# Splitting fp32 weights in tiles of 2048 columns instead of 1024, in a one-core transformer layer

## The chip, the cores and the metric

The kernel runs on one core of one Trainium2 chip. Its engines are TensorE (PE in the profile; PEld is its weight load), VectorE (DVE), ScalarE (ACT), GpSimd (POOL) and SyncE (SP), which issues most DMAs. Each engine takes its own instructions in the order in which they stand in the program, and waits at semaphores for the others. The metric is the device time of one execution in microseconds, lower is better; the time before is the median of three runs.

## The reference

One layer on 256 tokens of 2048 numbers, in fp32, batch 1, depth 1:

```python
x = x + 0.5 * swiglu(rmsnorm(x, ffn1_norm), ffn1_w_gate, ffn1_w_up, ffn1_w_down)   # 2048 -> 5632 -> 2048
h = rmsnorm(x, mix_norm)
rq, rk, rv, rg, aq, ak, av, iq, ik, iw = split(h @ w_in)
ro = group_norm(retention(rope(rq), rope(rk), rv)) * ret_norm * silu(rg)            # 8 heads of 128
ao = sparse_attention(rope(aq), rope(ak), av, rope(iq), rope(ik), iw)               # 8 heads, 64 keys of 256 kept
x = x + concat([ro, ao]) @ w_out
x = x + 0.5 * swiglu(rmsnorm(x, ffn2_norm), ffn2_w_gate, ffn2_w_up, ffn2_w_down)
return rmsnorm(x, final_norm)
# swiglu(h, g, u, d) = (silu(h @ g) * (h @ u)) @ d
```

All weights are fp32 and are read once from HBM, 356 MB in all.

## The kernel before

**Two halves of a number.** A product of fp32 matrices is made of three matmuls on rounded numbers: each operand is split into `hi` (the number rounded by a ScalarE copy to the type fp32r) and `lo` (the number minus `hi`, a VectorE subtraction), and hi·hi, hi·lo and lo·hi are summed in PSUM. So every weight that comes from HBM passes one copy on ScalarE (line 283) and one subtraction on VectorE (line 289) before TensorE can use it.

**Pairs.** A wide matrix product takes its weights in pairs: 256 rows by 1024 columns, laid out as one tile `raw` of 128 partitions by 2048 columns, that is four blocks of 512 columns; one DMA of 1 MB brings it (line 262). Three `raw` tiles exist, so a load waits until the tile three loads back has been read for the last time. A pair is of one of two kinds:

- A **C pair** is multiplied as it is: 4 blocks x 2 token halves x 3 = 24 matmuls of 512 columns.
- An **S pair** uses a scheme with seven products of 2 x 2 blocks instead of eight (the names A11, S1 to S4, M1 to M7 in the code): 7 x 3 = 21 matmuls. For it VectorE first makes four differences of blocks in place in `raw` (`less`, line 275), and the left operand needs sums of its blocks too (`blocks_of`).

The letters of `UP`, `PLAIN` and `DOWN` say which pairs are of which kind. In the order of execution the eight pairs of a usual chunk are S C S C S C C C.

**Stages.** Each FFN has 11 chunks (c0 to c10) of 512 gate and 512 up columns with 8 pairs each; c0 has C pairs alone. After c0 to c5 comes a first down part: 12 pairs for each of two halves d0 and d1 of the output; after c6 to c10 a second one with 10 pairs for each half. Between the FFNs stand the input projections of the mixer (`stream`, `cols`), its attention and retention, and w_out as two wide products, of which the first has three S pairs. At the end of a chunk the sums of the seven products are put together on VectorE (`sums_of`, `ups`, `hidden`; lines 473 and 555) with two SiLUs on ScalarE (line 552); eight TensorE transposes in the next chunk turn the result, and `left_pair` splits it for the down part.

**What sets the order.** The program is written out piece by piece. A piece is a part of a pair: two for a C pair, four for an S pair. The last loop of `layer` runs over the pieces: it calls `split` for pieces up to four ahead, then `run_step` (whatever `after` has put at that step, the sums and transposes among it), then the matmuls of the piece. The engines keep that order. Before the change `split` makes for each piece one `hi` and one `lo` tile of 1024 columns, of five each in turn:

```python
hi = new(wts, [P, 1024], F32R, "hi", BUFS)
lo = new(wts, [P, 1024], F32R, "lo", BUFS)
S.activation(hi[:, :p["n"]], raw, AF.Copy)
...
V.tensor_tensor(lo[:, :p["n"]], raw, hi[:, :p["n"]].bitcast(F32), op=OP.subtract)
```

In an S pair the four differences are put between these: one before the second piece's copy, two before its subtraction, one before the third piece's subtraction.

**Other places that the change touches.** `tables` makes the sine and cosine tables of the rotary embedding during the first down part of the first FFN: some 17 VectorE instructions for each of two tables, with `yield n` for "go on n pieces later". `turn_late` transposes the second half of x for the next stage. `cols("iq", ...)` is the first of the mixer's projections. `FIRST_SQ` and `first_x` belong to the start, where the pairs of x are split as they arrive.

Of the kernel before, what the change touches and what calls it, by code (L numbers as in the profile page):

```python
# [11 lines left out]
F32 = mybir.dt.float32  # L12
# [19 lines left out]
DOWN = ("SCSCSCSCCCCC", "SCSCSCSCCC")  # L32
# [5 lines left out]
BUFS = 5  # L38
# [12 lines left out]
def layer(ctx: ExitStack, tc: tile.TileContext, a: dict, out: bass.AP):  # L51
# [5 lines left out]
    mid = ctx.enter_context(tc.tile_pool(name="mid", bufs=16))  # L57
# [97 lines left out]
    def mm_rows(chunk, n, kts, rhs, first, last):  # L155
# [21 lines left out]

    def wide(src, plan, left, x0=False, tail=False, order=None, sums=SUM):
# [15 lines left out]
        for at, p in enumerate(order or range(len(plan))):  # L194
# [6 lines left out]
            if kind == "C":  # L201
                tiles = [(0, 1024), (1024, 1024)]
                if x0 and at == 0:
                    tiles = [(0, 512), (512, 512), (1024, 1024)]
            else:
                tiles = [(512, 1024), (1024, 1024), (0, 1024), (1536, 512)]
            for k, (off, n) in enumerate(tiles):
                pieces.append(dict(load=len(loads) - 1, off=off, n=n, mms=[], left=left, pair=p,
                                   sums=k if kind == "S" else None, x=[p] if x0 and k == 0 else []))
# [10 lines left out]
            else:  # L220
                for k, off, a, m in S_BLOCKS:
                    mm(i + k, off, a, m)
# [18 lines left out]
    def stream(src, kts, width, per_load, per_piece, rhs, chunk, maker, arg):  # L241

        n = len(kts)
        for l0 in range(0, n, per_load):
            l1 = min(n, l0 + per_load)
            loads.append([(0, block(src, l0, l1, width))])
            for k0 in range(l0, l1, per_piece):
                k1 = min(l1, k0 + per_piece)
                pieces.append(dict(load=len(loads) - 1, off=(k0 - l0) * width, n=(k1 - k0) * width,
                                   mm=maker(chunk, arg, kts[k0:k1], rhs, k0 == 0, k1 == n)))  # L250
# [12 lines left out]

    def split(i):
# [7 lines left out]
        raw = r[:, p["off"]:p["off"] + p["n"]]  # L272
# [249 lines left out]
    def ffn(which, norm, next_norm, last):  # L522
        wgu, wd = a[f"wgu{which}"], [a[f"wd{which}{j}"] for j in range(2)]
        c = 0
        for part, n in enumerate(PARTS):
            hs = {}
            marks[which, part] = len(pieces)
            for cc in range(n):
                plain = c == 0
                start, s_end, half, end = wide(wgu[c], PLAIN if plain else UP, left_of(xg if plain else xs),  # L530
                                               plain and which == 1, order=None if plain else ORDER)
# [41 lines left out]
            for d in range(2):  # L573
# [18 lines left out]
    def turn_late(end, norm, banks):  # L592

        for i, s in ((2, 0), (3, 0), (0, 1), (1, 1)):
            after(end + s, lambda i=i: turn_x(4 + i, norm, banks[i]))
# [49 lines left out]
    def tables():  # L645
        for k in range(2):
# [3 lines left out]
            yield 3  # L650
# [45 lines left out]
    after(marks[1, 0, "down"] + 6, tables)  # L696
# [60 lines left out]
    cols("iq", a["w_iq"], 4, True)  # L757
# [347 lines left out]
def _pairs(w, plans):  # L1105
# [3 lines left out]
    order = {"S": ((0, 1), (0, 0), (1, 1), (1, 0)), "C": ((0, 1), (1, 1), (0, 0), (1, 0))}  # L1109
    return np.stack([np.concatenate([np.stack([chunk[p][:, kt, c] for kt, c in order[plan[p]]], 1).reshape(-1)  # L1110
                                     for p in (ORDER if plan is UP else range(len(plan)))])
                     for chunk, plan in zip(t, plans)])


def _layout(i):
# [22 lines left out]
    arr["w_out"] = c(_pairs(np.concatenate([wo[D // 2:], wo[:D // 2]]), [UP, PLAIN]))  # L1138
# [18 lines left out]
```

## Time and profile before

| | |
|---|---|
| time, median of 3 runs | 1871.88 us (1871.86 to 1872.03) |
| the profiled execution: its time, its span | 1873.38 us, 1871.6 us |
| TensorE matmul busy | 1838.7 us (98%), 8643 matmuls |
| VectorE busy | 1647.2 us (88%) |
| ScalarE busy | 1074.0 us (57%) |
| subtractions (line 289), copies (line 283) | 859, 977.2 us; 859, 846.3 us |
| differences (line 275) | 380, 262.9 us |
| HBM read | 356 MB, 192 GB/s over the span |

The span is what the profiler recorded of one execution; some microseconds lie around it. "Busy" of TensorE is modelled at the matmuls' ends, so a stage's length and number of matmuls tell more than its share. "ACT hi L283" in a list of waits is the copy, "DVE lo L289" the subtraction; "<-" behind an idle time names what ended it.

### The profile page before, as it was taken

What the parts mean: (1) busy time and instruction counts of PE and PEld (TensorE: products, weight loads), DVE (VectorE), ACT (ScalarE), POOL (GpSimd) and SP (SyncE); (2) the same over time, 40 slices, a digit from 0 to 9 for tenths busy, and PEclk for the clock granted to TensorE, in tenths of its full rate; (3) what the DMA queues carried; (4) which work ended last, traced back from release to release, by engine and by line L of the source; (5) the groups of instructions that cost most, each with busy time, mean ns of one, the idle gap of its engine ahead of it and who ended that gap; (6) DMA issues with size and microseconds to landing.
All of it is one profiled execution on the core that took longest, in us unless ns stands there. A gap on an engine that the chain in (4) does not pass through costs nothing.

```text
span 1871.6 us, 22796 instructions
## 1 busy us (share of the span) xinstructions
PE 1838.7 (98%) x8643; PEld 1524.3 (81%) x8643; DVE 1647.2 (88%) x2122; ACT 1074.0 (57%) x1353; POOL 5.8 (0%) x15
## 2 busy tenths in 40 slices
PE   9999998999999999999999999999999999999997
PEld 7888786788888887888888888888888888888886
DVE  7999999989999997789865886799999889999997
ACT  7655554455555555656554565555565455565564
POOL 0000000000000000000000000000000000000000
PEclk9999999999999999999999999999999999999999
DMA  8545555555555454545444454554554555545454
GB/s 317 201 180 197 193 200 186 185 199 206 182 212 212 184 204 165 183 158 206 179 156 158 157 209 154 205 198 181 206 210 182 209 197 195 194 183 213 189 190 170
DMA packets 52365, 360.51 MB, mean 193 GB/s; under 512 B 5984, under 2 KB 5984, under 8 KB 9760
## 3 DMA queue, kind: packets, MB, share of 16 engines
q1 hardware_dynamic: 50976, 355.62, 51.2%
q10 hardware_dynamic: 864, 2.13, 0.3%
q8 instruction: 67, 1.10, 0.2%
q0 software_dynamic: 416, 1.32, 0.2%
q14 instruction: 42, 0.34, 0.1%
HBM read 356.42 MB, written 2.62 MB: 192 GB/s over the span
## 4 chain that ended last, share of the span: by engine, by line
PE 83%; DVE 11%; ACT 3%; issue 1%; DMA 1%; ACTq 0%; SPq 0%; DVEq 0%
PE M L235 66%; PE M L149 8%; DVE lo L289 6%; PE M L151 4%; ACT hi L283 2%; DVE raw L275 2%; PE M L562 1%; PE M L168 1%; PE M L167 1%; PE M L166 1%; DVE x L470 1%; DMA e<-in_xT 0%; PE M L820 0%; ACT sq L412 0%; DVE e L473 0%
## 5 line engine op out<-in xcount | busy, mean ns | idle before, releaser
L283 ACT ACTIVATE hi<-raw 128x1024 fp32r<-128x1024 f32 (+2 forms) x859 | 846.3, 1007 | 558.1 <-DVE raw L275 360.9
L289 DVE TENSOR_TENSOR lo<-raw,hi 128x1024 fp32r<-128x1024 f32 (+2 forms) x859 | 977.2, 1159 | 129.6 <-ACT hi L283 116.4
L235 PE MATMUL M<-hi,xg 128*128 128x512 f32 x2240 | 726.0, 390 | 0.2 <-ACT hi L283 0.2
L235 PE MATMUL M<-hi,mid 128*128 128x512 f32 x1690 | 529.1, 391 | 2.8 <-DVE e L987 1.6
L235 PEld LDWEIGHTS M<-hi,xg 128*128 128x128 f32 x2240 | 420.5, 188 | 87.4 <-ACT hi L283 0.4
L235 PE MATMUL M<-lo,xg 128*128 128x512 f32 x1120 | 437.9, 391 | 5.6 <-DVE lo L289 5.6
L235 PEld LDWEIGHTS M<-hi,mid 128*128 128x128 f32 x1690 | 317.9, 188 | 71.7 <-DVE e L987 2.0
L235 PE MATMUL M<-lo,mid 128*128 128x512 f32 x845 | 330.4, 391 | 4.5 <-DVE lo L289 4.5
L275 DVE TENSOR_TENSOR raw<-raw 128x512 f32<-128x512 f32 x380 | 262.9, 692 | 12.7
L235 PEld LDWEIGHTS M<-lo,xg 128*128 128x128 f32 x1120 | 210.3, 188 | 55.0 <-DVE lo L289 12.2
L149 PE MATMUL M<-xg,hi 128*128 128x512 f32 x688 | 244.5, 399 | 1.2 <-DVE xg L303 1.2
L235 PEld LDWEIGHTS M<-lo,mid 128*128 128x128 f32 x845 | 159.0, 188 | 40.4 <-DVE lo L289 8.1
L151 PE MATMUL M<-xg,lo 128*128 128x256 f32 x645 | 180.5, 280 | 0.0
L149 PEld LDWEIGHTS M<-xg,hi 128*128 128x128 f32 x688 | 128.2, 188 | 30.9 <-DVE xg L303 1.8
L235 PE MATMUL M<-hi,ext 128*128 128x512 f32 x360 | 141.2, 392 | 0.1
L151 PEld LDWEIGHTS M<-xg,lo 128*128 128x128 f32 x645 | 121.8, 189 | 0.7
L235 PEld LDWEIGHTS M<-hi,ext 128*128 128x128 f32 x360 | 67.5, 188 | 17.2 <-DVE s L473 3.7
L235 PE MATMUL M<-lo,ext 128*128 128x512 f32 x180 | 70.1, 390 | 0.0
L473 DVE TENSOR_TENSOR s<-s,M 128x512 f32<-128x512 f32 x98 | 65.6, 683 | 1.9 <-PE M L235 0.9
L552 ACT ACTIVATE s<-s,r_tok 128x512 f32<-128x512 f32 x40 | 27.1, 719 | 53.7 <-DVE s L473 53.7
L473 DVE TENSOR_TENSOR e<-s,M 128x512 f32<-128x512 f32 x58 | 39.7, 684 | 1.0
L734 ACT ACTIVATE b<-e 64x512 f32<-64x512 f32 (+2 forms) x46 | 28.2, 612 | 20.2 <-DVE e L720 19.7
(175 smaller groups left out, 933.6 us busy)
## 6 DMA issues: line engine op xcount, KB each, us to landing
raw<-in_wgu SPq DMA_DIRECT2D x175, 1024.0 KB, 4.8
raw<-in_wd SPq DMA_DIRECT2D x88, 1024.0 KB, 4.8
raw<-in_w_out SPq DMA_DIRECT2D x16, 1024.0 KB, 4.8
raw<-in_w_iq SPq DMA_DIRECT2D x8, 1024.0 KB, 4.8
raw<-in_w_aq SPq DMA_DIRECT2D x8, 1024.0 KB, 4.8
raw<-in_w_rk SPq DMA_DIRECT2D x8, 1024.0 KB, 4.9
raw<-in_w_rq SPq DMA_DIRECT2D x8, 1024.0 KB, 4.8
raw<-in_w_rv SPq DMA_DIRECT2D x8, 1024.0 KB, 4.8
```

The costliest lines, as they stand in the source:

```text
L149: TE.matmul(acc, lhsT=hi[:, c:c + P], rhs=r, start=st, stop=sp)
L151: TE.matmul(acc[:, T:], lhsT=lo[:, c:c + P], rhs=r[:, :T], start=False, stop=False)
L166: TE.matmul(o, lhsT=h, rhs=hi[:, i * n:(i + 1) * n], start=st, stop=False)
L167: TE.matmul(o, lhsT=h, rhs=lo[:, i * n:(i + 1) * n], start=False, stop=False)
L168: TE.matmul(o, lhsT=l, rhs=hi[:, i * n:(i + 1) * n], start=False, stop=sp)
L235: TE.matmul(bank[m], lhsT=p["left"](pair, a)[u], rhs=split_of[i][v][:, off:off + 512], start=st, stop=sp)
L275: V.tensor_tensor(r[:, o:o + 512], r[:, a:a + 512], r[:, b:b + 512], op=OP.subtract)
L283: S.activation(hi[:, :p["n"]], raw, AF.Copy)
L289: V.tensor_tensor(lo[:, :p["n"]], raw, hi[:, :p["n"]].bitcast(F32), op=OP.subtract)
L473: V.tensor_tensor(o, a, b, op=OP.add)
L552: S.activation(u[b], bank[SUM[b]] if plain else u[b], AF.Silu, scale=r_tok[norm][:, t:t + 1])
L734: S.activation(b[p0:p0 + w], q[p1:p1 + w], AF.Copy)
```

## The change

Line numbers of the kernel after are larger: the copy is L274, the subtraction L275, the difference L303, the sums L497, the SiLU L577 and the products behind it L580.

- `split` keeps `hi` and `lo` tiles of 2048 columns, three each in turn: one of each for a C pair, two for an S pair. A C pair gets two copies of 1024 columns and one subtraction of 2048. An S pair gets first two copies (1024 and 512) and one subtraction of 1536 columns, then all four differences, two copies of 1024 and one subtraction of 2048.
- `S_BLOCKS` names the tile that each of the seven products reads; the piece in which its matmuls stand is as before but for two that change places.
- The first down part has five S pairs among its twelve instead of four; the left operands take 17 `mid` buffers instead of 16.
- At the start, chunk c0 of the first FFN takes its pairs in the order FIRST, those that are C in later chunks first.
- `tables` has longer steps between its instructions and starts 5 pieces earlier; its results leave by a POOL DMA.
- The first two index chunks take their loads in turns, and `turn_late` runs one piece later before the mixer.
- The program is built with 4096 bytes of dynamic DMA scratch.

```diff
-DOWN = ("SCSCSCSCCCCC", "SCSCSCSCCC")
+FIRST = (0, 2, 4, 6, 7, 1, 3, 5)
+DOWN = ("SCSCSCSCSCCC", "SCSCSCSCCC")
-BUFS = 5
+AHEAD = 4
-    mid = ctx.enter_context(tc.tile_pool(name="mid", bufs=16))
+    mid = ctx.enter_context(tc.tile_pool(name="mid", bufs=17))
     S_BLOCKS = (
-        (0, 0, "A11", "M1"), (0, 512, "S4", "M3"),
-        (1, 0, "S3", "M7"), (1, 512, "A12", "M2"),
...
+        (0, 0, 512, "A11", "M1"), (0, 0, 1024, "S4", "M3"),
+        (1, 0, 1536, "A12", "M2"), (1, 1, 1024, "S3", "M7"),
...
-                tiles = [(512, 1024), (1024, 1024), (0, 1024), (1536, 512)]
+                tiles = [(0, 2048)] * 4
...
+    def halves_of(r, hi, lo, a, b):
+
+        for o in range(a, b, 1024):
+            S.activation(hi[:, o:min(b, o + 1024)], r[:, o:min(b, o + 1024)], AF.Copy)
+        V.tensor_tensor(lo[:, a:b], r[:, a:b], hi[:, a:b].bitcast(F32), op=OP.subtract)
+
+    def parts(key):
+        if key not in split_in:
+            split_in[key] = [new(wts, [P, 2048], F32R, h, 3) for h in ("hi", "lo")]
+        return split_in[key]
...
-        raw = r[:, p["off"]:p["off"] + p["n"]]
+        k = p.get("sums")
+        if k is None:
+            hi, lo = parts(p["load"])
+            a, b = p["off"], p["off"] + p["n"]
+            if not p.get("second"):
+                halves_of(r, hi, lo, a, 2048 if p.get("whole") else b)
+            split_of[i] = (hi[:, a:b], lo[:, a:b])
+            return
+        if k > 1:
+            return
+        hi, lo = parts((p["load"], k))
...
-        k = p.get("sums")
-        if k == 1:
+        if k == 0:
+            halves_of(r, hi, lo, 512, 2048)
+        else:
             less(0, 1024, 1024)
-        hi = new(wts, [P, 1024], F32R, "hi", BUFS)
-        lo = new(wts, [P, 1024], F32R, "lo", BUFS)
-        S.activation(hi[:, :p["n"]], raw, AF.Copy)
-        if k == 1:
             less(0, 512, 0)
             less(512, 1024, 512)
-        elif k == 2:
             less(1536, 512, 1536)
-        V.tensor_tensor(lo[:, :p["n"]], raw, hi[:, :p["n"]].bitcast(F32), op=OP.subtract)
+            halves_of(r, hi, lo, 0, 2048)
...
-                                               plain and which == 1, order=None if plain else ORDER)
+                                               plain and which == 1,
+                                               order=ORDER if not plain else FIRST if which == 1 else None)
...
-                    turn_late(end, next_norm, ("M2", "M4", "M3", "M8"))
+                    turn_late(end, next_norm, ("M2", "M4", "M3", "M8"), 1)
...
-            yield 3
+            yield 4
             V.tensor_copy(pf, pi)
...
-            nc.scalar.dma_start(rot_dram[:, 2 * k:2 * k + 2], ang)
+            G.dma_start(rot_dram[:, 2 * k:2 * k + 2], ang)
...
-    after(marks[1, 0, "down"] + 6, tables)
+    after(marks[1, 0, "down"] + 1, tables)
...
+        if first:
+            for l0 in (0, 8):
+                for c in range(2):
+                    ends_[c] = part(src[c], kts, 256, l0, l0 + 8, 4, rhs_x, chunks[c], mm_cols, 2)
...
-        ahead = 2 if i < 11 else BUFS - 1
+        ahead = 2 if i < 11 else AHEAD
```

On VectorE, at the start of chunk c3 of the first FFN, its first C pair and second S pair stand like this before (`raw` is the pair's tile, `lo` the result of a subtraction; x3 is three in a row):

```order
L555 SCALAR_TENSOR_TENSOR e_1164<-e_1164,r_tok_3_76,s_1102 128x512
L289 TENSOR_TENSOR lo_1249<-raw_1105,hi_1248 128x1024
L289 TENSOR_TENSOR lo_1259<-raw_1105,hi_1258 128x1024
L289 TENSOR_TENSOR lo_1271<-raw_1168,hi_1270 128x1024
L275 TENSOR_TENSOR raw_1168<-raw_1168 128x512 x3
L289 TENSOR_TENSOR lo_1282<-raw_1168,hi_1281 128x1024
L275 TENSOR_TENSOR raw_1168<-raw_1168 128x512
L289 TENSOR_TENSOR lo_1291<-raw_1168,hi_1290 128x1024
L289 TENSOR_TENSOR lo_1308<-raw_1168,hi_1307 128x512
```

and like this after:

```order
L580 SCALAR_TENSOR_TENSOR e_1073<-e_1073,r_tok_3_76,s_1014 128x512
L275 TENSOR_TENSOR lo_1152<-raw_1017,hi_1151 128x2048
L275 TENSOR_TENSOR lo_1171<-raw_1077,hi_1170 128x1536
L303 TENSOR_TENSOR raw_1077<-raw_1077 128x512 x4
L275 TENSOR_TENSOR lo_1182<-raw_1077,hi_1181 128x2048
L275 TENSOR_TENSOR lo_1220<-raw_1149,hi_1219 128x2048
```

The C pair's two subtractions have become one, the S pair's four have become two, and its four differences stand in one run between them.

On ScalarE, at the end of chunk c2, the copies of the next chunk's first S pair, the two SiLUs and the copies of its first C pair (`hi` is the result of a copy, `s` a gate sum) stand like this before:

```order
L283 ACTIVATE hi_1170<-raw_1082 128x1024
L283 ACTIVATE hi_1187<-raw_1082 128x1024
L283 ACTIVATE hi_1205<-raw_1082 128x1024
L283 ACTIVATE hi_1224<-raw_1082 128x512
L552 ACTIVATE s_1101<-s_1101,r_tok_3_76 128x512
L552 ACTIVATE s_1102<-s_1102,r_tok_3_76 128x512
L283 ACTIVATE hi_1248<-raw_1105 128x1024
L283 ACTIVATE hi_1258<-raw_1105 128x1024
```

and like this after:

```order
L274 ACTIVATE hi_1079<-raw_997 128x1024
L274 ACTIVATE hi_1079<-raw_997 128x512
L274 ACTIVATE hi_1096<-raw_997 128x1024 x2
L577 ACTIVATE s_1013<-s_1013,r_tok_3_76 128x512
L577 ACTIVATE s_1014<-s_1014,r_tok_3_76 128x512
L274 ACTIVATE hi_1151<-raw_1017 128x1024 x2
L274 ACTIVATE hi_1170<-raw_1077 128x1024
```

As before, the copies of the first C pair stand behind the SiLUs; what reads them on VectorE (lo_1152 above) is now one instruction behind both.

On VectorE, in the second half of chunk c2, the last subtraction of its last S pair and its three C pairs, with the first sum of the chunk (`s`) between, stand like this before:

```order
L275 TENSOR_TENSOR raw_928<-raw_928 128x512
L289 TENSOR_TENSOR lo_1028<-raw_928,hi_1027 128x1024
L289 TENSOR_TENSOR lo_1045<-raw_928,hi_1044 128x512
L289 TENSOR_TENSOR lo_1063<-raw_983,hi_1062 128x1024
L289 TENSOR_TENSOR lo_1073<-raw_983,hi_1072 128x1024
L289 TENSOR_TENSOR lo_1085<-raw_1005,hi_1084 128x1024
L289 TENSOR_TENSOR lo_1095<-raw_1005,hi_1094 128x1024
L473 TENSOR_TENSOR s_1102<-s_1101,M_12_85 128x512
L289 TENSOR_TENSOR lo_1108<-raw_1060,hi_1107 128x1024
```

and like this after:

```order
L303 TENSOR_TENSOR raw_861<-raw_861 128x512 x4
L275 TENSOR_TENSOR lo_943<-raw_861,hi_942 128x2048
L275 TENSOR_TENSOR lo_981<-raw_910,hi_980 128x2048
L275 TENSOR_TENSOR lo_1000<-raw_929,hi_999 128x2048
L497 TENSOR_TENSOR s_1014<-s_1013,M_12_85 128x512
L275 TENSOR_TENSOR lo_1020<-raw_978,hi_1019 128x2048
L342 TENSOR_TENSOR sq_1045<-b_1040 128x128
```

The three C pairs had six subtractions of 1024 columns, the last of them behind the left operand's instructions, and have three. The tile of the third C pair (`raw_1060`, now `raw_978`) is the one that the S pair (`raw_928`, now `raw_861`) had three loads before.

## Rows read from the trace of the kernel before

**Rows 1.** Windows by stage; us, then busy time and count by engine, clock, DMA.

```profile
core 0: us, PE busy (x) PEld busy (x) DVE busy (x) ACT busy (x) POOL busy (x), PEclk, DMA share, GB/s
10.00:17.00 7.00, 4.63 (x18) 3.10 (x18) 6.28 (x13) 6.34 (x12) 0.00 (x0) 1.00 1.00 407
53.91:96.30 42.39, 42.39 (x193) 35.17 (x191) 39.26 (x47) 25.44 (x29) 0.00 (x0) 1.00 0.54 198
139.39:182.57 43.18, 42.84 (x192) 35.02 (x191) 41.45 (x52) 25.18 (x29) 0.54 (x1) 1.00 0.53 198
268.99:341.97 72.98, 67.02 (x285) 53.97 (x284) 68.35 (x97) 34.63 (x38) 0.00 (x0) 0.95 0.49 177
341.97:406.40 64.43, 63.30 (x278) 51.65 (x276) 55.91 (x65) 32.60 (x35) 0.00 (x0) 1.00 0.55 201
406.40:447.88 41.48, 41.48 (x185) 34.35 (x183) 37.82 (x43) 22.49 (x23) 0.00 (x0) 1.00 0.53 202
447.88:490.27 42.39, 42.39 (x192) 35.18 (x191) 40.08 (x49) 25.60 (x29) 0.00 (x0) 1.00 0.54 198
1415.76:1479.22 63.46, 63.46 (x285) 52.63 (x284) 56.78 (x65) 34.54 (x37) 0.00 (x0) 1.00 0.55 200
1479.22:1541.78 62.56, 62.56 (x277) 51.80 (x276) 54.35 (x61) 32.78 (x33) 0.00 (x0) 1.00 0.55 202
1755.05:1808.39 53.34, 52.97 (x237) 43.46 (x236) 50.99 (x60) 30.06 (x34) 0.00 (x0) 1.00 0.54 197
1808.39:1861.00 52.61, 52.46 (x229) 42.45 (x227) 47.17 (x61) 28.90 (x41) 0.00 (x0) 1.00 0.45 160
```

**Rows 2.** Lines by form, whole span: busy us, mean ns, idle before, releasers.

```profile
L289 DVE TENSOR_TENSOR lo<-raw,hi 128x1024 fp32r<-128x1024 f32 x756 | 911.0, 1221 | 124.7 <-ACT hi L283 111.6
...
L289 DVE TENSOR_TENSOR lo<-raw,hi 128x512 fp32r<-128x512 f32 x97 | 66.4, 685 | 3.3 <-ACT hi L283 3.2
```

**Rows 3.** Timeline of VectorE, chunk c3: start, us, what, idle before.

```profile
144.90 2.35 DVE L289 TENSOR_TENSOR lo<-raw,hi 128x1024 fp32r<-128x1024 f32 x2
147.29 2.15 DVE L275 TENSOR_TENSOR raw<-raw 128x512 f32<-128x512 f32 x3
149.35 1.22 DVE L289 TENSOR_TENSOR lo<-raw,hi 128x1024 fp32r<-128x1024 f32 x1
150.61 0.69 DVE L275 TENSOR_TENSOR raw<-raw 128x512 f32<-128x512 f32 x1
151.22 5.31 DVE L289 TENSOR_TENSOR lo<-raw,hi 128x1024 fp32r<-128x1024 f32 x5
156.56 2.15 DVE L275 TENSOR_TENSOR raw<-raw 128x512 f32<-128x512 f32 x3
...
168.33 1.23 DVE L289 TENSOR_TENSOR lo<-raw,hi 128x1024 fp32r<-128x1024 f32 x1 [0.55 <-ACT hi L283]
...
175.81 1.22 DVE L289 TENSOR_TENSOR lo<-raw,hi 128x1024 fp32r<-128x1024 f32 x1
```

**Rows 4.** Timeline of ScalarE, chunk c3.

```profile
148.10 1.06 ACT L283 ACTIVATE hi<-raw 128x1024 fp32r<-128x1024 f32 x1 [2.47 <-DVE raw L275]
...
184.64 1.34 ACT L552 ACTIVATE s<-s,r_tok 128x512 f32<-128x512 f32 x2 [2.84 <-DVE s L473]
185.88 2.94 ACT L283 ACTIVATE hi<-raw 128x1024 fp32r<-128x1024 f32 x3
```

**Rows 5.** Waits of TensorE: us in total, times, longest.

```profile
PE M L235 <- DVE lo L289: 10.1, 24, 0.9
PE M L562 <- ACT s L478: 3.6, 1, 3.6
...
PE M L149 <- DVE xg L303: 1.2, 1, 1.2
```

**Rows 6.** DMA issues of the page: count, KB each, us to landing.

```profile
raw<-in_wgu SPq DMA_DIRECT2D x175, 1024.0 KB, 4.8
```

**Rows 7.** Windows behind the long wait of TensorE, columns as in rows 1.

```profile
313.50:316.50 3.00, 2.38 (x9) 1.97 (x10) 3.00 (x4) 1.78 (x4) 0.00 (x0) 0.50 0.89 317
```

More of the change, by code (lines that the diff above doesn't have):

```diff
@@ L205, in wide @@
             else:
-                tiles = [(512, 1024), (1024, 1024), (0, 1024), (1536, 512)]
+                tiles = [(0, 2048)] * 4
             for k, (off, n) in enumerate(tiles):
-                pieces.append(dict(load=len(loads) - 1, off=off, n=n, mms=[], left=left, pair=p,
+                whole = kind == "C" and n == 1024 and k == 0
+                pieces.append(dict(load=len(loads) - 1, off=off, n=n, mms=[], left=left, pair=p, whole=whole,
+                                   second=kind == "C" and n == 1024 and k == 1 and len(tiles) == 2,
                                    sums=k if kind == "S" else None, x=[p] if x0 and k == 0 else []))
@@ L220, in wide @@
             else:
-                for k, off, a, m in S_BLOCKS:
-                    mm(i + k, off, a, m)
+                for k, b, off, a, m in S_BLOCKS:
+                    mm(i + b, off, a, m, i + k)
                 s_end = len(pieces)
@@ L244, in stream, with part @@
         for l0 in range(0, n, per_load):
[L245 to L250, printed above, removed]
+            part(src, kts, width, l0, min(n, l0 + per_load), per_piece, rhs, chunk, maker, arg)
+        return len(pieces)
+    def part(src, kts, width, l0, l1, per_piece, rhs, chunk, maker, arg):
+        loads.append([(0, block(src, l0, l1, width))])
+        for k0 in range(l0, l1, per_piece):
+            k1 = min(l1, k0 + per_piece)
+            pieces.append(dict(load=len(loads) - 1, off=(k0 - l0) * width, n=(k1 - k0) * width,
+                               mm=maker(chunk, arg, kts[k0:k1], rhs, k0 == 0, k1 == len(kts))))
         return len(pieces)
     n_loaded = [0]
+    split_in = {}
     def load(i):
@@ L590, in turn_early, with turn_late @@
             after(s_end + 2 + i, lambda i=i, m=m: turn_x(i, norm, m))
-    def turn_late(end, norm, banks):
+    def turn_late(end, norm, banks, later=0):
         for i, s in ((2, 0), (3, 0), (0, 1), (1, 1)):
-            after(end + s, lambda i=i: turn_x(4 + i, norm, banks[i]))
+            after(end + s + later, lambda i=i: turn_x(4 + i, norm, banks[i]))
     def finish(ready):
@@ L737, in rope, with cols @@
         V.tensor_tensor(dst, q, b, op=OP.add)
-    def cols(name, src, nchunks, idx=False):
+    def cols(name, src, nchunks, idx=False, first=False):
         heads[name] = []
+        kts, ends_ = list(range(KT)), {}
+        chunks = [Chunk() for _ in range(nchunks)]
+        if first:
+            for l0 in (0, 8):
+                for c in range(2):
+                    ends_[c] = part(src[c], kts, 256, l0, l0 + 8, 4, rhs_x, chunks[c], mm_cols, 2)
         for c in range(nchunks):
-            chunk = Chunk()
-            end = stream(src[c], list(range(KT)), 256, 8, 4, rhs_x, chunk, mm_cols, 2)
+            chunk = chunks[c]
+            end = ends_[c] if c in ends_ else stream(src[c], kts, 256, 8, 4, rhs_x, chunk, mm_cols, 2)
             def done(chunk=chunk, c=c):
@@ L1102, in _tiles, with _pairs @@
     return np.concatenate(parts, 1)
-def _pairs(w, plans):
+def _pairs(w, plans, orders):
     k, n = w.shape
     t = w.reshape(k // 256, 2, P, n // 1024, 2, 512).transpose(3, 0, 2, 1, 4, 5)
[L1109 to L1112, printed above, removed]
+    blocks = {"S": ((0, 1), (0, 0), (1, 1), (1, 0)), "C": ((0, 1), (1, 1), (0, 0), (1, 0))}
+    return np.stack([np.concatenate([np.stack([chunk[p][:, kt, c] for kt, c in blocks[plan[p]]], 1).reshape(-1)
+                                     for p in order or range(len(plan))])
+                     for chunk, plan, order in zip(t, plans, orders)])
 def _layout(i):
```

26 lines of the change are left out of this document (15 added, 11 removed), and 4 rows, old and new, of the table S_BLOCKS.

## The prediction

> **What bounds the kernel now.** I read the stages first [rows 1]. Chunk c6 has no transposes: 183 matmuls in 41.48 us without a pause, so a 512-column matmul costs TensorE 0.2267 us; c7 has 8 transposes more and takes 42.39, again without a pause. The steady chunk c3 takes 43.18, 0.8 more than TensorE needs, and the waits name what ends that time: 24 waits for L289's subtraction, 10.1 us in all [rows 5]. VectorE is busy for 41.45 of those 43.18 us. Its timeline shows how thin the margin is [rows 3]: from the first difference of one S pair (147.29) to that of the next (156.56) lie one S and one C pair back to back, 9.27 us, where TensorE needs 21 + 24 matmuls, 10.20 us. So TensorE bounds the kernel by 0.9 us per S+C, and over a whole chunk, with the sums and the left operands, VectorE already does. A microsecond added to VectorE per S pair is a microsecond of the kernel.
>
> **The split.** In wide() 3 or 4 subtractions per S pair become 2, and 2 per C pair become 1. From 512 to 1024 columns a subtraction grows from 685 to 1221 ns [rows 2], 1.047 ns a column on 149 ns; 1536 columns then take 1.76 us, 2048 take 2.29. (No row has these widths; the bounds are 2.14 without any fixed part and 2.44 as two of 1024; I take the line through both rows.) Of the fixed part 0.08 us already overlaps: two subtractions of 1024 follow each other in 2.35 - 1.22 = 1.13 us [rows 3]. A C pair costs VectorE 2.27 now and 2.21 then.
>
> [...]
>
> [...] Now (first and second order blocks; 147.29 to 152.4 in [rows 3]) differences and subtractions alternate, so that each ScalarE copy lies beside another VectorE instruction. Afterwards the four differences stand together and the subtraction right behind them needs both 1024-column copies of their results; nothing stands between, and VectorE works in order. From the start of the first subtraction: it ends at 1.76; differences follow at 0.73 each ((2.15 - 0.69)/2), the third ends at 3.94; ScalarE starts 0.12 later (difference done at 147.98, copy at 148.10 [rows 4]), its second copy 0.94 behind the first ((2.94 - 1.06)/2), done at 6.06; the subtraction runs 6.08 to 8.37, and the next instruction starts at 8.29. The fourth difference was done at 4.66: 1.4 us idle. An S pair costs VectorE 8.29 instead of 9.27 - 2.27 = 7.00, +1.3 us, on 99 pairs; S+C becomes 10.50, over TensorE's 10.20.
>
> **A whole chunk, followed along VectorE** from the end of the last S pair's second subtraction (time 0):
> - Three C pairs. The raw tile of the third is the S pair's own (three buffers), so its load is issued at 0.1 and lands 4.8 later [rows 6]; both copies 2.0; subtraction 7.07 to 9.36. The two other subtractions and one sum fill only 5.0: 2 us idle (0.55 now [rows 3], where the first half could start alone).
> - Left operands and three sums: now from the end of the subtraction at 168.33 (169.56) to 175.81, with one subtraction in between [rows 3]: 6.25 - 1.13 = 5.1, of which I take 4.9 as work: 14.25.
> - First S pair of the next chunk: 8.37 more, 22.6.
> - Three sums of 512 columns to the first gate sum, 0.69 - 0.08 each as the difference at 150.61 [rows 3], end 24.4; two SiLUs and then the copies of the next C pair, which start 1.24 after the first SiLU (184.64 to 185.88 [rows 4]), 2.0 for both, then 2.29: 30.0. Now the first half's subtraction goes after one copy.
> - S, C, S: 8.29 + 2.21 + 8.37: 48.8.
>
> 48.8 against 43.18 is +5.6 us per chunk; TensorE waits some 4.7 us of it at that first C pair, the rest in the S pairs. c2 to c5 and c8 to c10 are such chunks: 14 x 5.6 = 78.4. c1 has no left operands before it and comes from a chunk without S: by the same steps 44.7 against 42.39, and c6, behind a down part, 42.4 against 41.48, c7 47.0 against 42.39: 2 x (2.3 + 0.9 + 4.6) = 15.6.
>
> **Down parts.** On the same scale TensorE begins the first half at 20.0 (2.6 for the last 11 matmuls of the S pair, 16.4 for three C pairs, 1.0 for the transposes). The first C is done at 30.0, the second S at 38.3, the fifth three S+C later at 69.8; 2.6 + 16.4 + 1.0 more and 0.5 for a late left operand end the half at 90.3, 70.3 long (63.46 now). The second half, from its predecessor's last S pair: 9.4 for the C pairs, 1.2 left operands, 2.0 sums, 2.4 additions into x, first S 23.3, four more additions and the first C 27.9, fifth S 67.7, end 86.7, less 20.5: 66.2 (62.56 now). Together +10.5 in the second FFN. In it lies the gain of the extra pair: 12 matmuls in all, 2.7 us of TensorE, which pays only where TensorE is the bound; on VectorE each such pair costs 8.29 - 2.27 = 6.0. In the first FFN the tables are on VectorE too: 68.35 + 55.91 against 56.78 + 54.35 [rows 1], 13.1 us. Spreading them moves none off VectorE; bounds 0 (they fill its waits) and 13.1, and since VectorE is the bound in both halves then, I take 13.1: 136.5 + 13.1 = 149.6 against 137.4, +12.2. The shorter down part: first half 59.8 against 53.34, +6.4 twice; second half by the same steps 55.7 against 52.61, +3, twice (half of it a guess in the first FFN, where the transposes for the mixer lie in it). w_out has three S pairs: +2, as c1.
>
> **The rest.** At the start the C pairs now come first, so less is made of x before the second pair: TensorE idles 2.4 us between 10 and 17 [rows 1]; bounds -2.4 and +1 (a 2048-column tile is ready later), I take -2. Interleaved index columns and transposes a step later: the wait for xg before the projections is 1.2 us [rows 5]; -1.2 to +1, I take -1. 17 mid buffers, tables written by POOL, the smaller scratch: none of the waits in the rows is for POOL, 0, within 1 us either way.
>
> Sum: 78.4 + 15.6 + 10.5 + 12.2 + 12.8 + 6 + 2 - 3 = 134.5. The profiled execution took 1873.4 us (1871.6 of span), so 2008; the median of the runs is 1.5 lower: **2006 us**.
>
> **Rivals.**
> 1. Faster. The wait for the copies falls into time in which VectorE waits for buffers anyway, and fewer instructions count. Then 2.7 for the matmuls, the 10.1 of waits for subtractions, 2.4 at the start and 1.2 at the projections go: 1855. For it: ScalarE waits for TensorE's buffers now, and VectorE has 1.7 us idle per chunk. Against: it would need 1.4 us of free wait behind every S pair, 4.2 per chunk. It decides if an S+C stays under 10.20 on VectorE. 0.06; no change (its gain and a small stall cancel) 0.02.
> 2. Only the added wait counts: loads, SiLUs and tables hide in it. A chunk then takes VectorE's own 41.45 + 3 x 1.3 - 5 x 0.07 + 0.7 of small waits = 45.7, +2.5 in 14 chunks, 8 in the others, 8.5 and 12 in the long down parts, 13 in the short, -3: 1945. For it: ScalarE is idle nearly half of a chunk. Against: copies stand behind the SiLUs in ScalarE's order. 0.2.
> [...]
>
> **Numbers.** Forecast 0.52, rivals 0.06, 0.2 and 0.2, no change 0.02. The range reaches over rivals 2 and 3: 1935 to 2045, with about 0.1 below and 0.05 above. A measurement of this kernel tells 0.2%, about 3.7 us, from no change. Faster 0.06, same 0.02, slower 0.92.
>
> **What would show it.** Right: behind L303's four differences VectorE idles about 1.4 us, ended by L274's copy, 99 times; steady chunks near 48.8; VectorE less busy in total, yet TensorE waiting for L275's subtraction above 100 us; copies of the third C pair ended by a load. [...] Wrong: chunks near 43, or the copies done before the fourth difference ends, which the order excludes unless the copies start on less than it shows.

## The result, and the profile after

The changed kernel takes **2035.95 us** (median of 4 runs, 2035.03 to 2036.87) against 1871.87: a ratio of 1.0876, 95% interval 1.0863 to 1.0889. It is slower by 164 us, where 134 were predicted (2006, range 1935 to 2045).

The stages of the changed kernel, in windows with the columns of [rows 1]; in order c1, c3, c5, the two halves of the long down part, c6 and c7 of the first FFN, then w_out's first half, and the long down part and c6 of the second FFN:

```profile
55.55:104.67 49.12, 45.19 (x193) 36.00 (x192) 39.44 (x38) 28.44 (x34) 0.00 (x0) 0.97 0.46 171
153.35:201.93 48.58, 45.37 (x192) 35.72 (x191) 40.55 (x40) 24.34 (x30) 0.00 (x0) 0.96 0.46 173
250.49:299.07 48.58, 43.86 (x193) 34.79 (x192) 40.59 (x40) 24.24 (x30) 0.00 (x0) 1.00 0.46 174
299.07:375.52 76.45, 69.15 (x283) 53.53 (x281) 66.44 (x71) 34.34 (x41) 1.08 (x2) 0.96 0.47 170
375.52:449.31 73.79, 66.60 (x275) 52.65 (x274) 63.92 (x67) 31.62 (x37) 0.55 (x1) 0.95 0.49 175
449.31:496.79 47.48, 43.84 (x184) 35.07 (x183) 38.16 (x32) 22.26 (x25) 0.00 (x0) 0.96 0.48 177
496.79:543.48 46.69, 43.85 (x193) 34.79 (x191) 38.83 (x40) 24.30 (x29) 0.00 (x0) 1.00 0.48 180
1147.49:1197.66 50.17, 45.04 (x188) 35.66 (x187) 41.33 (x39) 25.09 (x30) 0.00 (x0) 0.97 0.52 189
1529.03:1599.28 70.25, 66.62 (x283) 52.42 (x281) 59.27 (x53) 34.20 (x40) 0.00 (x0) 0.98 0.49 180
1599.28:1667.42 68.14, 64.96 (x274) 52.00 (x273) 56.73 (x49) 32.14 (x36) 0.00 (x0) 0.97 0.50 185
1667.42:1714.65 47.23, 43.94 (x184) 35.26 (x183) 38.21 (x32) 21.59 (x24) 0.00 (x0) 0.96 0.49 178
```

The steady chunk c3 takes 48.58 instead of 43.18 [rows 1]. Read its VectorE column beside the length: VectorE works less than before (40.55 against 41.45) and idles 8.0 us of the chunk where it idled 1.7. The work went down; the chunk grew by waiting.

The lines by form show the same over the whole span: the merged subtractions, and how long VectorE sat idle ahead of them:

```profile
L275 DVE TENSOR_TENSOR lo<-raw,hi 128x2048 fp32r<-128x2048 f32 x279 | 632.0, 2290 | 253.0 <-ACT hi L274 244.6 <-PE M L238 8.5
L303 DVE TENSOR_TENSOR raw<-raw 128x512 f32<-128x512 f32 x396 | 274.1, 692 | 13.3
L275 DVE TENSOR_TENSOR lo<-raw,hi 128x1536 fp32r<-128x1536 f32 x99 | 173.5, 1752 | 8.5 <-ACT hi L274 8.5
```

The 2048-column subtraction takes 2290 ns and the 1536-column one 1752, as the line through the two widths of [rows 2] gave (2.29 and 1.76). But 245 us of idle time stand ahead of the wide ones, put down to ScalarE's copy; ahead of the 1024-column ones of before it was 112 [rows 2].

Where it lies, the timeline of VectorE in c3 shows (in brackets the idle time before a row, and what ended it; answers to [rows 3]):

```profile
153.55 2.29 DVE L275 TENSOR_TENSOR lo<-raw,hi 128x2048 fp32r<-128x2048 f32 x1 [1.41 <-PE M L238]
...
160.93 3.96 DVE L275 TENSOR_TENSOR lo<-raw,hi 128x2048 fp32r<-128x2048 f32 x2 [1.09 <-ACT hi L274]
164.93 2.87 DVE L303 TENSOR_TENSOR raw<-raw 128x512 f32<-128x512 f32 x4
169.23 6.16 DVE L275 TENSOR_TENSOR lo<-raw,hi 128x2048 fp32r<-128x2048 f32 x3 [1.43 <-ACT hi L274]
175.42 2.88 DVE L303 TENSOR_TENSOR raw<-raw 128x512 f32<-128x512 f32 x4
179.73 6.70 DVE L275 TENSOR_TENSOR lo<-raw,hi 128x2048 fp32r<-128x2048 f32 x3 [1.43 <-ACT hi L274]
...
188.85 2.29 DVE L275 TENSOR_TENSOR lo<-raw,hi 128x2048 fp32r<-128x2048 f32 x1 [1.82 <-ACT hi L274]
```

Three times the four differences stand in one run, and behind each run VectorE idles 1.4 us. The first of the three is named as a wait for TensorE; that it is as long as the others (1.41) says that the copies end it too, e2 below names them at this place, again with 1.41, and e1 takes it away with the others. Then there are the two places of the C pairs: 1.09 behind the SiLUs, 1.82 at the third C pair. In ScalarE's timeline the copies of that third pair wait for its load:

```profile
186.81 2.01 ACT L274 ACTIVATE hi<-raw 128x1024 fp32r<-128x1024 f32 x2 [2.39 <-DMA raw<-in_wgu]
```

The waits of TensorE, against [rows 5]. (The row of the weight load, PEld, has 83.6 us for L275. These are the same 52 waits again, each some 0.4 us longer, and 44 more of at most 0.54 us beside which no matmul is listed as waiting: in c3 one wait stands as 0.39 at the matmul and 0.81 at its weight load. So the two rows can't be added.)

```profile
PE M L238 <- DVE lo L275: 43.3, 52, 2.0
PE M L238 <- DVE e L497: 42.8, 20, 2.4
PE M L238 <- DVE x L494: 17.9, 11, 3.3
```

Only the first of these three, 10.1 us before, was expected to grow. The other two are waits for a PSUM bank that VectorE has not yet read out (L497 and L494 read `M`, the sums in PSUM). How they share out a chunk shows in c5:

```profile
253.62 0.50 PE L238 MATMUL M<-hi,xg 128*128 128x512 f32 x1 [2.29 <-DVE e L497]
...
260.40 0.50 PE L238 MATMUL M<-lo,xg 128*128 128x512 f32 x1 [1.63 <-DVE lo L275]
```

The first is at the start of the chunk, the second at its first C pair; two more waits, of 0.33 and 0.48, make up the 4.72 us that TensorE idles in c5 (48.58 less 43.86).

### The profile page after: what moved, and what is told of

It reads as the page before. It is cut to its first block, busy times and chain, and to the rows that moved or that the text cites. A ratio compares the mean times of both kernels' runs of the same rounds, so it can differ in the third digit from the quotient of the medians.

```text
span 2035.0 us, 22180 instructions
## 1 busy us (share of the span) xinstructions
PE 1902.5 (93%) x8631; PEld 1537.9 (76%) x8631; DVE 1632.5 (80%) x1778; ACT 1048.3 (52%) x1365; POOL 6.9 (0%) x17
## 5 line engine op out<-in xcount | busy, mean ns | idle before, releaser
L275 DVE TENSOR_TENSOR lo<-raw,hi 128x2048 fp32r<-128x2048 f32 (+4 forms) x489 | 932.1, 1933 | 303.1 <-ACT hi L274 294.3
L274 ACT ACTIVATE hi<-raw 128x1024 fp32r<-128x1024 f32 (+1 forms) x867 | 818.4, 998 | 678.6 <-DVE raw L303 509.1
L238 PE MATMUL M<-hi,xg 128*128 128x512 f32 x2240 | 737.5, 396 | 41.7 <-DVE e L497 33.3
L238 PE MATMUL M<-hi,mid 128*128 128x512 f32 x1682 | 540.4, 399 | 25.0 <-DVE x L494 11.6
L238 PEld LDWEIGHTS M<-hi,xg 128*128 128x128 f32 x2240 | 427.2, 191 | 137.9 <-DVE e L497 40.1
L238 PE MATMUL M<-lo,xg 128*128 128x512 f32 x1120 | 447.9, 400 | 24.9 <-DVE lo L275 24.6
L238 PEld LDWEIGHTS M<-hi,mid 128*128 128x128 f32 x1682 | 322.8, 192 | 101.9 <-DVE x L494 11.8
L238 PE MATMUL M<-lo,mid 128*128 128x512 f32 x841 | 338.0, 402 | 19.0 <-DVE lo L275 18.7
L303 DVE TENSOR_TENSOR raw<-raw 128x512 f32<-128x512 f32 x396 | 274.1, 692 | 13.3
L238 PE MATMUL M<-hi,ext 128*128 128x512 f32 x360 | 146.8, 408 | 5.7 <-DVE s L497 3.9
L577 ACT ACTIVATE s<-s,r_tok 128x512 f32<-128x512 f32 x40 | 26.7, 715 | 83.1 <-DVE s L497 83.1
L497 DVE TENSOR_TENSOR s<-s,M 128x512 f32<-128x512 f32 x98 | 65.3, 683 | 1.0
L497 DVE TENSOR_TENSOR e<-s,M 128x512 f32<-128x512 f32 x58 | 39.6, 683 | 1.0
L238 PEld LDWEIGHTS M<-lo,ext 128*128 128x128 f32 x180 | 35.1, 195 | 6.4
```

The source lines that it names most:

```text
L238: TE.matmul(bank[m], lhsT=p["left"](pair, a)[u], rhs=split_of[i][v][:, off:off + 512], start=st, stop=sp)
L274: S.activation(hi[:, o:min(b, o + 1024)], r[:, o:min(b, o + 1024)], AF.Copy)
L275: V.tensor_tensor(lo[:, a:b], r[:, a:b], hi[:, a:b].bitcast(F32), op=OP.subtract)
L303: V.tensor_tensor(r[:, o:o + 512], r[:, a:a + 512], r[:, b:b + 512], op=OP.subtract)
L497: V.tensor_tensor(o, a, b, op=OP.add)
L577: S.activation(u[b], bank[SUM[b]] if plain else u[b], AF.Silu, scale=r_tok[norm][:, t:t + 1])
```

## The experiments

Theory: VectorE, working in order, waits for copies that used to lie beside its own work. Rivals: the coarse tiles and buffers; the late C pairs alone; TensorE's banks or clock. The first five runs take back one part of the changed kernel or two; the next three take back three parts more, one after the other; the last does one part of the change alone.

**e1, the S pairs' order undone.** Each copy is issued right behind its differences (`copy(a, b)` is the copy of columns a to b, `rest(a, b)` their subtraction), and the subtraction is cut in three.

```diff
...
             less(0, 1024, 1024)
+            copy(1024, 1536)
             less(0, 512, 0)
             less(512, 1024, 512)
+            copy(0, 1024)
             less(1536, 512, 1536)
-            halves_of(r, hi, lo, 0, 2048)
+            copy(1536, 2048)
+            rest(1024, 1536)
+            rest(0, 1024)
+            rest(1536, 2048)
```

> One thing undone: the order inside an S pair's second tile. The copy of a quarter is issued right behind its difference, and the one subtraction of 2048 becomes 512 + 1024 + 512, so that each copy lies beside another VectorE instruction. Tiles of 2048, three buffers, the order of pairs, the extra S pair and the tables stay. Theory (VectorE idles 1.4 us behind the four differences because the subtraction needs both copies): that idle time goes, two subtractions more cost 0.15 each, so an S pair costs VectorE some 1.2 us less; a steady chunk 48.6 -> 45.0 (44.5 to 45.5), the kernel 2036 -> some 1923 (1910 to 1940). Rival A (the coarse tiles and three buffers are the cause, the wait would only move to another place): chunk above 47.5, kernel above 2000. Rival B (the late first C pair and the third C pair's load alone set the chunk): chunk 48.6 less at most 0.5, kernel above 2020.

Measured: 1932.1 us (ratio to before 1.0319, 1.0304 to 1.0335), 104 us back; the steady chunks take 45.43 on average. VectorE in c3:

```profile
158.78 2.87 DVE L303 TENSOR_TENSOR raw<-raw 128x512 f32<-128x512 f32 x4
161.57 2.42 DVE L313 TENSOR_TENSOR lo<-raw,hi 128x512 fp32r<-128x512 f32 x3
164.77 3.96 DVE L275 TENSOR_TENSOR lo<-raw,hi 128x2048 fp32r<-128x2048 f32 x2 [0.78 <-ACT hi L274]
```

The idle time behind the differences is gone (161.57 follows without a bracket), with tiles and buffers unchanged: rivals A and B fall. (The edit changes two things, the place of the copies and the cut of the subtraction; e5 changes the copies alone.) It is not all gained, for the C pair behind now idles 0.78, as its two copies stand behind the S pair's in ScalarE's order.

**e2, the C pairs' subtraction in halves again.**

```diff
-                whole = kind == "C" and n == 1024 and k == 0
+                whole = False
-                                   second=kind == "C" and n == 1024 and k == 1 and len(tiles) == 2,
+                                   second=False,
```

> One thing undone: the C pairs' subtraction of 2048 is two of 1024 again, each behind its own copy. The S pairs stay as changed. Theory (a C pair's merged subtraction waits for both copies where they come late: behind the SiLUs, and on the third C pair, whose tile is loaded late): of 48.6 us per steady chunk 1.0 comes back at the third C pair and 0.9 at the first C pair behind the SiLUs, five more subtractions cost 0.07 each: chunk some 46.9 (46.4 to 47.5), kernel some 1998 (1985 to 2012). Rival (these waits lie in slack, the S pairs alone make the time): chunk 48.6 +0.3, kernel 2036 to 2050.

Measured: 1996.09 us (1.0665, 1.0649 to 1.0680), 40 us back; steady chunks 47.31. The two places, to be read against 160.93 and 188.85 of the changed kernel:

```profile
155.20 4.17 DVE L275 TENSOR_TENSOR lo<-raw,hi 128x1024 fp32r<-128x1024 f32 x3 [0.15 <-ACT hi L274]
...
182.54 1.23 DVE L275 TENSOR_TENSOR lo<-raw,hi 128x1024 fp32r<-128x1024 f32 x1 [0.83 <-ACT hi L274]
```

1.09 became 0.15 and 1.82 became 0.83; less the 5 x 0.07 of more subtractions that is 1.6, of which 1.3 reach the end of the chunk. The first chunk of the first FFN, c0, which has C pairs alone, takes 45.5 instead of 48.6; c1 then takes 49.96 instead of 49.11, so 2.3 of these 3.1 are left.

**e3, both.**

> Both orders undone: S pairs' second tile interleaved and C pairs' subtraction in halves. Tiles, buffers, order of pairs, extra S pair, tables and scratch stay as changed. Theory (all of the loss is waiting for copies in VectorE's order): chunk 43.0 to 43.8, kernel 1865 to 1890, about the kernel before. Rival (two causes overlap, or the rest of the change has a cost of its own: three 2048 buffers, the product that holds a bank, the extra S pair): above 1900.

Measured: 1880.19 us (1.0043, 1.0026 to 1.0060), 156 us of the 164 back, more than 104 and 40 together: with the halves, e1's new idle time at the C pairs goes too (VectorE waits for L274's copies 106.1 us in all, 184.9 in e1). Windows: c0, c1 and c3 of the first FFN, c6 of the first and of the second:

```profile
6.67:52.56 45.89, 44.58 (x195) 35.91 (x194) 34.43 (x60) 34.96 (x65) 0.00 (x0) 1.00 0.79 302
52.56:102.46 49.90, 45.61 (x192) 36.94 (x191) 43.50 (x54) 29.65 (x38) 0.00 (x0) 0.93 0.50 181
145.62:188.83 43.21, 42.89 (x192) 35.02 (x191) 41.20 (x52) 25.04 (x32) 0.00 (x0) 1.00 0.52 195
...
408.17:453.98 45.81, 43.63 (x185) 35.36 (x184) 40.99 (x48) 22.28 (x28) 0.00 (x0) 0.96 0.53 187
1549.80:1591.28 41.48, 41.48 (x185) 34.31 (x184) 38.19 (x44) 21.81 (x26) 0.00 (x0) 1.00 0.56 206
```

The steady chunk is that of before. Two stages stay late: c1, and c6 in the first FFN; e6 and e7 are for them.

**e4, four S pairs in the long down parts.** `DOWN = ("SCSCSCSCCCCC", "SCSCSCSCCC")` on the changed kernel.

> One thing undone: the extra S pair in the long down parts (SCSCSCSCCCCC again, 12 matmuls more in each long down part's two halves together, 24 matmuls in all over two FFNs). All else stays as changed. Theory (with S pairs that wait for copies S+C costs VectorE 10.5 and C+C costs TensorE 10.9, so the fifth S pair is worth nothing): 2036 within 6 us either way. Rival (each extra S pair costs VectorE 6.0 us more than a C pair, as the prediction put it, and VectorE sets the time): four of them, 24 us, come back: 2012. Second rival (TensorE sets the time in the down parts, 12 matmuls of 0.227 in each half's place): 2 x 5.4 slower, 2047.

Measured: 2013.58 us (1.0760, 1.0744 to 1.0776), 22 us back. The theory fell here and the rival, the prediction's own 6.0 per pair on VectorE, held: four pairs, 24. (The expectation counts too many matmuls: it is 3 more in each of the four halves, 283 to 286 in the first, and 12 in all. So the second rival would be 2.7 us slower, 2039, and falls as well.) Windows of the two halves and of c6 in the first FFN:

```profile
299.16:372.93 73.77, 67.72 (x286) 53.14 (x285) 63.30 (x68) 33.28 (x38) 1.08 (x2) 0.98 0.50 176
372.93:442.25 69.32, 64.36 (x278) 51.25 (x277) 59.56 (x64) 30.83 (x35) 0.55 (x1) 1.00 0.51 186
442.25:484.64 42.39, 42.09 (x185) 34.13 (x183) 35.19 (x30) 21.19 (x23) 0.00 (x0) 1.00 0.54 199
```

The halves lose 2.7 and 4.5 against the changed kernel, and c6 loses 5.1: more than half of the second half's price is paid in the chunk behind it, which stands at the 42.4 of the prediction once the pair is gone.

**e5, a smaller dose.** The four differences and the one subtraction stay in one run; only ScalarE's copies are cut in four, each issued behind its own difference.

```diff
-            less(0, 1024, 1024)
-            less(0, 512, 0)
-            less(512, 1024, 512)
-            less(1536, 512, 1536)
-            halves_of(r, hi, lo, 0, 2048)
+            for a, b, o in ((0, 1024, 1024), (0, 512, 0), (512, 1024, 512), (1536, 512, 1536)):
+                less(a, b, o)
+                S.activation(hi[:, o:o + 512], r[:, o:o + 512], AF.Copy)
+            V.tensor_tensor(lo, r, hi.bitcast(F32), op=OP.subtract)
```

> A smaller dose of the same cause. In an S pair's second tile each difference of 512 columns is followed at once by its own copy of 512 on ScalarE; the four differences stay in one run and the one subtraction of 2048 stays behind them, so VectorE issues what the changed kernel issues, in the same order. Theory (the idle time behind the differences is the rest of the last copies: 0.12 to start one, 0.63 for 512 columns instead of 1.06 + 0.94 for two of 1024): VectorE idles 0.75 instead of 1.43 behind the differences, 99 x 0.68 = 67 less at most, of which the two thirds to three quarters that the interleaved version gave of its own should reach the end: chunk 48.6 -> 46.9, kernel 1980 (1965 to 1995). Rival (the cost is one of the wide VectorE subtraction itself, or of the three buffers): no change, above 2025.

Measured: 1974.83 us (1.0550, 1.0533 to 1.0566), 61 us back; steady chunks 46.72.

```profile
159.50 2.87 DVE L303 TENSOR_TENSOR raw<-raw 128x512 f32<-128x512 f32 x4
163.07 2.29 DVE L312 TENSOR_TENSOR lo<-raw,hi 128x2048 fp32r<-128x2048 f32 x1 [0.70 <-ACT hi L311]
```

VectorE issues the same instructions as in the changed kernel in the same order, and idles 0.70 instead of 1.43. With 99 pairs, 1.43, 0.70 and 0 idle give 2036, 1975 and 1932: the time follows the idle time (the last of the three has two subtractions more in each pair), and the wide subtraction, which e5 leaves as it is, is not the cause of these 61 us.

**e6, e7, e8: three parts more.** Each adds one edit to the version before it, starting from e3: the first chunk's pairs in plain order (e6); four S pairs in the long down parts (e7); tables at the old places, in the old steps, stored by ScalarE's queue (e8).

> The version with both orders undone, and the first chunk's pairs in plain order again (0 to 7, instead of 0, 2, 4, 6, 7, 1, 3, 5). Theory (the S operands made of x for pairs 1, 3, 5 now come at the end of the first chunk and delay chunk c1: 49.9 there against 42.4 for c1 of the second FFN): c0 + c1 go from 95.4 to about 89.8, kernel 1880.2 -> 1874.6 (1872 to 1877). Rival (c1 is late because three 2048 buffers start late, not through the order): c0 + c1 stay above 94, kernel 1879 to 1882.

> The version before this one (both orders and the start undone), and in the long down parts four S pairs again instead of five. Theory (the fifth S pair puts c6 of the first FFN behind additions into x, 45.8 there instead of 41.5, and gives TensorE less than VectorE takes from it): another 4 to 6 us go: 1869.5 (1867 to 1872), faster than the kernel before by its spread tables. Rival (with the waits for copies gone TensorE bounds, and the extra S pairs' 12 matmuls in each long part are worth 2.7 each): 1879 to 1881.

> As the version before this one, with the tables of positions made at the places and in the steps of the kernel before, and stored by ScalarE's queue. Theory (the spread tables save the 5.3 us by which the first FFN's first long half is shorter, 67.7 against 73.0, now that TensorE waits for no copies there): 5 us slower than the version before this one, about the kernel before, 1872 to 1876. Rival (that gain comes from the four steps ahead or from the merged first subtraction, not from the tables): within 1.5 us of the version before this one.

Measured: 1874.11 (1.0009, 1.0000 to 1.0017), 1869.88 (0.9986, 0.9977 to 0.9995) and 1878.89 (1.0037, 1.0024 to 1.0049). In e6, c0 and c1:

```profile
6.49:53.23 46.74, 44.77 (x193) 35.98 (x193) 39.08 (x66) 39.26 (x72) 0.00 (x0) 1.00 0.82 315
53.23:95.62 42.39, 42.39 (x193) 35.18 (x192) 39.09 (x47) 24.98 (x32) 0.00 (x0) 1.00 0.54 198
```

The new order of the first chunk saves 0.85 in c0 (45.89 in e3) and costs 7.5 in c1. The block sums of x that an S pair needs as left operand are made when its pair comes up in c0; the three pairs that are S later now come up last, so this work reaches into c1. VectorE's column shows it, 34.4 in c0 and 43.5 in c1 with the new order, 39.1 in both without. In e7, c6 of the first FFN is 41.48 again (44.32 in e6), so the fifth S pair is worth less than it costs even where the orders are undone. (The rival's 5.4 us counts matmuls twice here too; with 12 in all it would be 1877.) That c6, and the two halves of the first FFN's long down part, in e7 and then in e8:

```profile
398.73:440.21 41.48, 41.48 (x185) 34.35 (x184) 37.54 (x43) 21.80 (x26) 0.00 (x0) 1.00 0.55 204
268.53:335.36 66.83, 64.28 (x286) 52.45 (x284) 63.02 (x83) 33.92 (x42) 1.08 (x2) 1.00 0.54 195
335.36:398.73 63.37, 63.20 (x278) 51.60 (x277) 60.30 (x79) 31.70 (x39) 0.55 (x1) 1.00 0.55 203
```

```profile
269.07:343.39 74.32, 67.83 (x285) 54.36 (x284) 68.26 (x96) 34.41 (x42) 0.00 (x0) 0.95 0.49 173
343.39:408.98 65.59, 63.71 (x277) 51.49 (x276) 55.97 (x66) 31.89 (x39) 0.00 (x0) 1.00 0.53 198
```

With the tables spread, VectorE has 5.2 us less to do in the first half and 4.3 more in the second, which has room for it, and the two halves together are 9.7 us shorter; 5 were expected, and e8's time lies above its range, in the direction of the theory.

e8 has both orders, the start, the fifth S pair and the tables undone, and is still 6.2 us slower than the kernel before (1.0037, 1.0024 to 1.0049). What it keeps of the change is the tiles of 2048 in three buffers with an S pair's subtractions cut otherwise (1536, 512, 1024, 512), the order of the index loads, the later transposes, the 17 `mid` buffers and the scratch; no run takes these apart.

**e9, the tables alone**, on the kernel before:

```diff
-            yield 3
+            yield 4
...
-            nc.scalar.dma_start(rot_dram[:, 2 * k:2 * k + 2], ang)
+            G.dma_start(rot_dram[:, 2 * k:2 * k + 2], ang)
...
-    after(marks[1, 0, "down"] + 6, tables)
+    after(marks[1, 0, "down"] + 1, tables)
```

> The kernel before with one part of the change alone: the tables of positions are begun five steps earlier, spread over twice as many steps, and stored by POOL's queue. Tiles of 1024, order of pairs and all else are those of before. Theory (the tables are hidden where TensorE bounds: in the first FFN's long down part they cost 11.4 us more than the second FFN's in the kernel before, 4.1 in the version with four S pairs, so 7 to 9 go): 1872.7 -> 1864.5 (1862 to 1867). Rival (VectorE is the bound there, as the prediction took it, and moving its work within the part frees nothing): 1870 to 1874.

Measured: **1864.24 us** (0.9961, 0.9947 to 0.9974), faster than both kernels. The same two halves:

```profile
268.17:334.58 66.41, 64.25 (x286) 52.38 (x284) 62.93 (x83) 34.37 (x38) 1.08 (x2) 1.00 0.55 197
334.58:397.85 63.27, 63.19 (x277) 51.64 (x276) 60.37 (x79) 32.12 (x35) 0.55 (x1) 1.00 0.56 204
```

72.98 and 64.43 [rows 1] became 66.41 and 63.27: 7.7 us, the whole gain. Start, steps and store were moved together; which of them gives it was not tried. e7, which has these tables and what e8 keeps of the change, gains 2.8 us on the kernel before, so that remainder costs 4.9 us here too.

## Why the prediction was right, and what its sum missed

| term | predicted | measured |
|---|---|---|
| 14 steady chunks | +78.4 | +76.1 |
| c1, c6, c7, twice each | +15.6 | +28.5 |
| long down part, second FFN | +10.5 | +12.4 |
| the same, first FFN (tables) | +12.2 | +12.8 |
| short down parts, first halves | +12.8 | +12.7 |
| their second halves, with the projections | +5 | +11.2 |
| w_out | +2 | +6.2 |
| second FFN's c0 | 0 | +1.9 |
| start and c0 of the first FFN | -2 | +1.7 |
| sum | +134.5 | +163.5 |

(Measured: the difference of the stages in the two profiled executions. In the second row the two chunks c6 alone are +11.8 where +1.8 stood.)

- **The S pair: right.** 1.4 us of idle time behind each run of differences was worked out from ScalarE's copies beside the differences; 1.40 to 1.43 is measured behind all 99, e5 and e1 show that it carries the time, and the steady chunk came at 48.6 for 48.8. (An S pair had four subtractions before, not "3 or 4"; nothing rests on it.)
- **The C pairs: right in place, a little large.** 2 us at the third C pair, 1.82 measured; both places together give 1.3 per chunk, where e2 was expected to free 1.7. e2 takes both away at once; no run separates the load from the SiLUs.
- **Fewer subtractions.** 489 in place of 859. One of 2048 columns takes 2.29 us, two of 1024 in a row take 2.35 [rows 3]. VectorE's busy time fell by 15 us (1647.2 to 1632.5), and the kernel lost 164.
- **The fifth S pair: right in price, wrong in place.** 6.0 a pair, 22 us for four (e4). The sum laid the second half's share inside that half, and took c6 at 42.4, as if the C pairs at the end of a part gave VectorE time to catch up. This is the step that failed: the two c6 together are 10 us later than in the sum, and with four S pairs they are at 42.4 (e4). At the start of c6 TensorE waits for the additions into x, and these stand behind the next S pair's subtraction in VectorE's order:

```profile
450.53 2.29 DVE L275 TENSOR_TENSOR lo<-raw,hi 128x2048 fp32r<-128x2048 f32 x1 [1.43 <-ACT hi L274]
452.74 2.48 DVE L494 SCALAR_TENSOR_TENSOR x<-M,x 128x512 f32<-128x512 f32 x4
...
453.48 0.50 PE L238 MATMUL M<-hi,xg 128*128 128x512 f32 x1 [3.33 <-DVE x L494]
```

Of the 5.1 us by which this c6 is longer than e4's, 3.3 are this wait and 1.8 are longer matmuls at a lower clock (43.84 against 42.09, clock 0.96 against 1.00). With four S pairs the waits for L494 fall from 17.9 to 5.7 us over the kernel. That the place of the additions is the way in which the pair costs c6 was not tried by itself.

- **The start: wrong sign.** The step "less is made of x before the second pair" counted only what leaves the beginning. What leaves c0 lands in c1: 4.4 us more there than predicted, and 7.5 where the orders are undone (e6). And c0 itself, all C pairs, paid 3.1 for their merged subtraction (e2), which the sum bounded at +1.
- **Second halves, w_out and the second FFN's c0: sized by analogy, too small.** e1 brings w_out's first half to 45.84 (44.23 before, 50.17 changed) and takes 8.1 of the 11.2 off the second halves; e2 brings the second FFN's c0 to 44.54, as before. So these are mostly the same two waits, in stages that were not followed step by step.
- **TensorE's wait: right in size, wrong in place.** The forecast had 4.7 us of it per chunk at the first C pair, and over 100 us in all for L275's subtraction. TensorE idles 4.72 in c5, but only 1.63 of it at the first C pair and 2.29 for the bank at the start of the chunk. So L275 has 43.3 us in all, and L497 another 42.8.
- **Tables: right for the changed kernel, and only there.** The part with tables costs 11.8 more than the one without (150.2 against 138.4), for the 13.1 taken: both halves wait for VectorE. Where the second half is bound by TensorE (busy for 63.19 of its 63.27 us in e9), spreading them is worth 7.7 to 9.7 (e9, e8).
- **Rival 1** (faster) falls with the result. **Rival 2** (only the added wait, chunk 45.7, 1945) falls with the chunk of 48.6 and with e2, where the C pairs' waits are worth 40 us. **Rival 3** (the clock): the granted clock does fall, to 0.51 in c4 of the first FFN, and costs nothing in the steady chunks (below); for the odd stages no run shows its price. The top of the range, 2045, reaches over this rival by the author's estimate of that price.

## What to carry to other kernels

Before merging instructions into a wider one, ask what the engine did between them: if its operand comes from another engine that was working beside it, the merged instruction waits for the whole of that work. Here a subtraction less saved VectorE 0.07 to 0.15 us ([rows 2], [rows 3]), and each S pair, with two fewer, paid 1.43 us of waiting. Follow such an edit along the engine's own order through every kind of stage, the short and odd ones too; here the steady chunks came out within 3% and the odd stages held the whole error. And an edit that moves work out of one stage has to be charged where the work lands: the first chunk's order and the fifth S pair were both paid in the chunk behind.

## What the runs showed of the hardware

The granted clock fell behind some waits of TensorE: to 0.50 in the kernel before [rows 7], to 0.51 in the changed one. In the steady chunks, which VectorE bounds, the fall cost nothing. Windows of the changed kernel: a stretch of c4 at the end of a wait of 2.26 us, the whole of c4, and, to set beside it, c5 (shown above), where the clock stayed at 1.00 behind a wait of 2.29:

```profile
204.70:208.20 3.50, 3.17 (x8) 2.37 (x9) 3.31 (x6) 1.99 (x3) 0.00 (x0) 0.51 0.71 262
...
201.93:250.49 48.56, 45.03 (x193) 35.80 (x192) 40.55 (x40) 24.28 (x30) 0.54 (x1) 0.96 0.48 176
```

In the stretch the granted clock is 0.51, and the matmuls start 0.43 us apart (205.62 to 207.33), where they start 0.23 apart behind c5's wait (255.21 to 255.89). TensorE is busy for 1.2 us more in c4 than in c5 (45.03 against 43.86), and the two have the same length, 48.56 and 48.58: the slow matmuls fill time that TensorE would have waited, and its wait at the first C pair is 0.75 instead of 1.63. All 14 steady chunks say the same. Each has a wait of 2.25 to 2.40 us near its start; behind it the clock falls in nine of them (a mean of 0.79 to 0.82 over the 8 to 10 us from the chunk's start), which average 48.62 us from the end of this wait to the next chunk's, and stays at 1.00 in the other five, which average 48.64.

This is shown for the steady chunks alone. The first half of the first FFN's long down part has a mean clock of 0.95 in the kernel before and 1.00 in e9. TensorE's busy time there is 67.02 and 64.25 us, 2.8 of the 6.6 us by which the half is shorter in e9; what the clock alone is worth in it, no run shows.
